# A four-block sequence model on one core: elementwise products on another engine, 512 weight columns per matmul, parameter rows in another order

## The chip, the cores and the metric

The kernel runs on one core of a Trainium2 chip. The core has a matrix engine (TensorE, PE in the rows; its weight loads are PEld), a vector engine (VectorE, DVE), an activation engine (ScalarE, ACT), a general engine (GpSimd, POOL) and SyncE (SP), which here only issues transfers. Each engine has a queue of its own and takes its instructions in order; engines wait for one another by semaphores. SBUF is the on-chip memory that all of them read; TensorE writes its results to PSUM, a second, smaller memory. The metric is the device time of one execution in microseconds.

## What is computed

The input `x` is 256 tokens of 1024 features, in fp32. It goes through two blocks of a first kind and two of a second; all weights are fp32 and are read from HBM once. The reference, cut to its core:

```python
# first kind, for i in 0, 1
proj = rmsnorm(x, norm_mix[i]) @ w_in[i]             # q k v cb cc cx u g
y_attn = sliding_window_attention(q, k, v, sinks) @ w_attn_o[i]
y_conv = (cb * short_conv(cc * cx, conv_w[i])) @ w_conv_o[i]
ys = gelu(s5_ssm(u, ...));  y_ssm = (ys * sigmoid(ys @ w_ssm_glu[i])) @ w_ssm_o[i]
x = x + (g0 * y_attn + g1 * y_conv + g2 * y_ssm) @ w_mix_o[i]
x = x + (silu(gt) * up) @ w_ffn_out[i]               # gt, up = rmsnorm(x) @ w_ffn_in[i]
# second kind, for l in 0, 1
u = rmsnorm_2(h, norm_mix_w[l]) @ w_in[l]            # q k v g_ret z xbc dt gate_ret gate_ssd
yr = retention(rotary(q), rotary(k), v);  o_ret = (silu(g_ret) * norm(yr)) @ ret_out[l]
xs, bm, cm = split(silu(causal_dwconv(xbc)))
lmat[i, j] = exp(acs[i] - acs[j]) for j <= i         # acs: running sum of dt * a
y = ((cm @ bm.T) * lmat) @ (xs * dt) + (state part) + d_skip * xs
o_ssd = (norm(y * silu(z)) * ssd_norm_w) @ ssd_out[l]
h = h + (sigmoid(gate_ret) * o_ret + sigmoid(gate_ssd) * o_ssd) @ w_o[l]
h = h + (silu(gate) * up) @ w_down[l]                # swiglu
# at the end: rmsnorm_2(h, final_norm_w)
```

## The kernel before

Every large product is made of three products of a reduced format (fp32r): weights and activations are each split into a high part and the rest (`wh`, `wl`; `xh`, `xl`, or `hh`, `hl` and the like), and `wh*xh + wh*xl + wl*xh` is summed in PSUM. Weights stream in chunks of 512 KB (`chunk`): SP issues the transfer into one of four `raw` buffers, ACT copies it to `wh` (L121 in the rows, the line of the activation helper), DVE subtracts to get `wl` (L96, the line of the two-tensor helper; L108 is that of the scalar-tensor-tensor helper `stt`). There are five buffers for the split weights.

Two functions make the products. `fm` gives a feature-major result: 128 weight columns are loaded into the array, the 256 tokens stream past. `tm` gives a token-major result: 128 tokens are loaded into the array and the weight columns stream past, 256 of them at a time. In the rows a `tm` matmul reads `mm<-wh,xh`, an `fm` matmul `mm<-xh,wh`, and both have an output of 128x256. In PSUM there are four `mm` buffers of 128x512 values for these and three `ax` buffers of the same size for all else. `tm` makes, in the first blocks, k and v (one product) and q; in the second blocks v and the gate `sg` of each of the four retention heads, `z` of each of the four groups of the SSD stage, and the last FFN product in `output`.

Small chains (rotations, attention, retention heads, the SSD groups' tails, the state-space tables) are generators that `bg.tick()` advances between products. A scheduler then sets the final order of each engine's queue from the dependences, so what is written in a row need not stand in a row.

The SSD stage runs once per second block, over four groups: two `fm` products for `xs`, one `tm` pair for `z` (its silu is `silu2`, L1066), `cb_step` (L1297), the gate product, `xd_step` (L1307) and, later, `group_tail`. `cb_step` multiplies the mask `cbm` into the two decay matrices `Lm` (each 128 x 4 x 384) of the group on POOL; ACT has made these by exponentials before. `xd_step` turns `xs` with TensorE transposes (L1315) into PSUM (`px`), copies that to SBUF with ACT, and has POOL multiply it by dt (`xd`) and by d_skip (`xD`). POOL thus works from SBUF only.

Parameters: `s5_params` loads four small arrays for the state space on ACT's queue at the start. `more_params` is called from `early2` in the first block, after the k/v product: it loads four sets of rows on SP's queue, each followed by a transpose (L190) and a copy into `vec` (L191). The products of the first block need `gfirst` alone at the start; the conv, the gates and the sinks need the rows.

`output` makes the last product in four parts of 256 columns. For each part DVE adds the residual (`xt`), ACT sums squares, POOL multiplies by the gain (`og`); a root on DVE and a last scaling follow.

## Time and profile before

| | us |
|---|---|
| median of 3 runs (2308.11 to 2315.36) | 2312.09 |
| the profiled execution, its span | 2316.8 |
| TensorE busy in it | 2231.6 |
| VectorE busy | 1562.6 |
| ScalarE busy | 1189.4 |
| GpSimd busy | 329.1 |

The span goes from the first to the last instruction of the profiled execution; nothing is measured around it. It stands 4.7 us above the median of the runs. A row of a timeline has the start in us, the duration, engine, line, operation and tiles; a number in square brackets is the time that the engine stood idle before it, with what released it. Rows of matmuls have modelled ends: a matmul's recorded duration is longer than the distance to the next one's start, and it is the distance that counts. Stretches: the first blocks run to about 940 us, the retention and SSD stages of the second blocks at about 950 to 1350 and 1630 to 2050, each followed by its FFN.

### The profile page before, as it was taken

The page shows a single profiled execution, that of the slowest core. Times are in us where ns is not written, and L with a number is a line of the kernel's source. Part 1 is how long each engine was busy: PE and PEld are TensorE (multiplying, and loading weights), DVE is VectorE, ACT ScalarE, POOL GpSimd, SP SyncE. Part 2 cuts the span into 40 slices and gives each one's busy share as a digit, 9 for nine tenths or more (in the row PEclk, how much of TensorE's full clock was granted, in tenths as well). Part 3 has the DMA queues.
Part 4 walks back from the last instruction along what each step waited for, and adds up shares of the span by engine and source line. Part 5 has one row for each costly group of instructions (what it writes and reads, how often), then busy time and mean ns, then how long its engine had stood idle before and what let it go on. Part 6 is the DMA issues. An engine that isn't in the chain of part 4 may idle for free. (4 is left out here: it accounts for less than half of the span.)

```text
span 2316.8 us, 44580 instructions
## 1 busy us (share of the span) xinstructions
PE 2231.6 (96%) x18211; PEld 2199.0 (95%) x18211; DVE 1562.6 (67%) x2533; ACT 1189.4 (51%) x1837; POOL 329.1 (14%) x441
## 2 busy tenths in 40 slices
PE   6899999999999999999999999999999999999998
PEld 6889999999999999999999989999999999989998
DVE  7676686658757665866577867665766577867654
ACT  6556555645555444444476735444444466645443
POOL 5720074101000000100022210000100022310001
PEclk8999999999999999999999999999999999999999
DMA  6333657677456556555576546656555665546553
GB/s 182 119 101 118 184 178 226 221 222 246 140 146 195 182 179 183 164 165 168 161 211 177 150 143 186 183 177 186 161 167 151 196 186 162 152 154 191 182 168 115
DMA packets 409410, 398.27 MB, mean 172 GB/s; under 512 B 28357, under 2 KB 407157, under 8 KB 408181
## 3 DMA queue, kind: packets, MB, share of 16 engines
q1 hardware_dynamic: 408324, 394.59, 56.6%
q8 instruction: 142, 2.33, 0.4%
q10 hardware_dynamic: 880, 0.84, 0.1%
q14 instruction: 64, 0.52, 0.1%
HBM read 386.92 MB, written 8.45 MB: 171 GB/s over the span
## 5 line engine op out<-in xcount | busy, mean ns | idle before, releaser
L96 DVE TENSOR_TENSOR wl<-raw,wh 128x1024 fp32r<-128x1024 f32 (+1 forms) x700 | 890.1, 1274 | 505.8 <-ACT wh L121 501.7
L121 ACT ACTIVATE wh<-raw 128x1024 fp32r<-128x1024 f32 (+1 forms) x700 | 725.8, 1043 | 831.8 <-PE mm L127 706.4
L127 PE MATMUL mm<-xh,wh 128*128 128x256 f32 (+1 forms) x2960 | 850.1, 287 | 3.9 <-ACT wh L121 1.4
L127 PE MATMUL mm<-xl,wh 128*128 128x256 f32 (+1 forms) x2960 | 844.8, 286 | 0.6 <-DVE xl L108 0.6
L127 PE MATMUL mm<-xh,wl 128*128 128x256 f32 (+1 forms) x2960 | 844.3, 285 | 0.2 <-DVE wl L96 0.2
L127 PEld LDWEIGHTS mm<-xh,wh 128*128 128x128 f32 (+1 forms) x2960 | 572.6, 194 | 7.1 <-ACT wh L121 2.3
L127 PEld LDWEIGHTS mm<-xl,wh 128*128 128x128 f32 (+1 forms) x2960 | 572.7, 194 | 2.1 <-issue 1.0
L127 PEld LDWEIGHTS mm<-xh,wl 128*128 128x128 f32 (+1 forms) x2960 | 572.2, 193 | 2.2 <-issue 1.3
L127 PE MATMUL mm<-wh,xh 128*128 128x256 f32 x864 | 252.4, 292 | 0.2 <-DVE tb L96 0.2
L127 PE MATMUL mm<-wh,xl 128*128 128x256 f32 x864 | 246.7, 286 | 5.9 <-DVE xl L108 5.9
L127 PE MATMUL mm<-wl,xh 128*128 128x256 f32 x864 | 245.3, 284 | 0.1
L127 PE MATMUL mm<-y,wh 128*128 128x256 f32 x1024 | 184.5, 283 | 0.0
L127 PEld LDWEIGHTS mm<-wh,xl 128*128 128x128 f32 x864 | 166.8, 193 | 10.1 <-DVE xl L108 7.1
L127 PEld LDWEIGHTS mm<-wh,xh 128*128 128x128 f32 x864 | 166.8, 193 | 3.2 <-issue 1.4
L127 PEld LDWEIGHTS mm<-wl,xh 128*128 128x128 f32 x864 | 166.5, 193 | 0.4 <-DVE wl L96 0.3
L127 PEld LDWEIGHTS mm<-y,wh 128*128 128x128 f32 x1024 | 157.2, 188 | 0.5 <-ACT wh L121 0.4
L96 POOL TENSOR_TENSOR Lm<-Lm,cbm 128x1536 f32<-128x1536 f32 x16 | 65.5, 4114 | 623.4 <-DMA raw<-in_w_in_dram 462.0
L127 PE MATMUL mm<-hh,wh 128*128 128x256 f32 x528 | 148.5, 281 | 0.0
L127 PE MATMUL mm<-hh,wl 128*128 128x256 f32 x528 | 148.1, 280 | 0.0
L127 PE MATMUL mm<-hl,wh 128*128 128x256 f32 x528 | 148.0, 280 | 0.0
L127 PE MATMUL mm<-y,wl 128*128 128x256 f32 x512 | 144.0, 281 | 0.0
L127 PEld LDWEIGHTS mm<-hh,wl 128*128 128x128 f32 x528 | 100.0, 189 | 0.0
(354 smaller groups left out, 3136.7 us busy)
## 6 DMA issues: line engine op xcount, KB each, us to landing
raw<-in_w_in_dram SPq DMA_DIRECT2D x284, 512.0 KB, 3.8
raw<-in_w_ffn_in_dram SPq DMA_DIRECT2D x88, 512.0 KB, 3.7
raw<-in_w_gate_up_dram SPq DMA_DIRECT2D x88, 512.0 KB, 3.6
raw<-in_w_ffn_out_dram SPq DMA_DIRECT2D x40, 512.0 KB, 4.4
raw<-in_w_down_dram SPq DMA_DIRECT2D x40, 512.0 KB, 3.5
raw<-in_ret_out_dram SPq DMA_DIRECT2D x32, 512.0 KB, 4.0
raw<-in_ssd_out_dram SPq DMA_DIRECT2D x32, 512.0 KB, 3.5
raw<-in_w_mix_o_dram SPq DMA_DIRECT2D x16, 512.0 KB, 3.6
```

The source lines that it names most:

```text
L96: return eng.tensor_tensor(out=o, in0=a, in1=b, op=op)
L121: return SC.activation(out=o, in_=i, func=f, **kw)
L127: return PE.matmul(out=o, lhsT=l, rhs=r, start=start, stop=stop)
```

## The change

- `tm` streams 512 weight columns per matmul in place of 256, with two `mm` buffers per product (one per half of the tokens); a chunk for it holds 2 x 512 columns in place of 4 x 256, the same bytes. The k/v product keeps 256. The callers that made two products of 256 make one of 512, and a step of the side chains that stood between the two stands in its middle (`mid`).
- In the SSD stage the `Lm`, `xd` and `xD` products go from POOL to DVE, and `xd` and `xD` read PSUM directly, so the ACT copy goes.
- The first row set and the sinks are loaded at the start, on ACT's queue behind the state-space arrays (`load_params_1`); the three other sets and `drow` later, on SP's queue (`load_params_2`), and they are turned separately (`params_1`, `params_2`).
- High and low parts lie in one tile (`xhl`, `pair`). `silu2` works in place, per token half. `output` makes two parts of 512 columns. In the second blocks the norm's `finish` and the rotation of the first head follow the whole v product, where they stood after its first half.

```diff
-    def more_params(q):
-        for i in range(4):
-            load_rows(i, stg[:, 258 + 128 * i:386 + 128 * i], q)
-        q.dma_start(out=sinks, in_=A["attn_sinks"].partition_broadcast(128))
-        q.dma_start(out=drow, in_=A["d_skip_2"].partition_broadcast(128))
...
+    def load_params_1(q):
...
+        load_rows(0, q)
+        q.dma_start(out=sinks, in_=A["attn_sinks"].partition_broadcast(128))
+    def params_1():
+        turn_rows(0)
...
+    def load_params_2(q):
+        for i in (1, 2, 3):
+            load_rows(i, q)
+        q.dma_start(out=drow, in_=A["d_skip_2"].partition_broadcast(128))
+    def params_2():
+        for i in (1, 2, 3):
+            turn_rows(i)
...
-        for k0 in range(0, KT, 4):
-            kn = min(4, KT - k0)
+        step = 2 if n == 512 else 4
+        for k0 in range(0, KT, step):
+            kn = min(step, KT - k0)
...
-    def tm(w, c0, K, xh, xl, n=256):
-        ps = mmt()
+    def tm(w, c0, K, src, n=512, mid=None):
+        if n == 512:
+            ps = [mmt().rearrange("p a s -> p (a s)") for _ in range(2)]
+        else:
+            both = mmt()
+            ps = [both[:, b, 0:n] for b in range(2)]
...
-                    mmu(ps[:, b, 0:n], h_, wh[:, k, 0:n], kt == 0 and b == 0, False)
-                    mmu(ps[:, b, 0:n], l_, wh[:, k, 0:n], False, False)
-                    mmu(ps[:, b, 0:n], h_, wl[:, k, 0:n], False, kt == KT - 1 and b == 1)
+                    mmu(ps[b], h_, wh[:, k, :], kt == 0 and first, False)
+                    mmu(ps[b], l_, wh[:, k, :], False, False)
+                    mmu(ps[b], h_, wl[:, k, :], False, kt == KT - 1 and last)
+            if mid is not None and k0 + kn == KT // 2:
+                mid()
...
-            for mp in range(4):
-                ps = tm(w_out, mp * 256, FH, hh, hl)
+            for mp in range(2):
+                ps = tm(w_out, mp * 512, FH, hid)
...
             for t in Lms[g]:
-                mul(t, t, bc(cbm, 4), G)
+                mul(t, t, bc(cbm, 4))
...
-                xt = T(tmp, [128, 2, S], "ta").rearrange("p a (h e) -> p (a h) e", e=64)
-                cp(xt, px.rearrange("p (h e) -> p h e", h=8))
-                mul(xd[:, b], xt, bl(dth[:, b, hs], 64), G)
-                mul(xD[:, b], xt, bl(drow[:, l, hs], 64), G)
+                xt = px.rearrange("p (h e) -> p h e", h=8)
+                mul(xd[:, b], xt, bl(dth[:, b, hs], 64))
+                mul(xD[:, b], xt, bl(drow[:, l, hs], 64))
```

The order of the instructions on three engines shows what the diff alone doesn't. A row has the line, the operation, the output and the inputs, the output's size and, on some, the semaphores that it waits for. First TensorE's queue at the v product of the first retention head of the last block, before:

```order
L127 MATMUL mm_19608<-wh_19611,xh_92 128x256
L127 MATMUL mm_19608<-wh_19611,xl_93 128x256
L127 MATMUL mm_19608<-wl_19612,xh_92 128x256
L127 MATMUL mm_19608<-wh_19611,xh_92 128x256
L127 MATMUL mm_19608<-wh_19611,xl_93 128x256
```

And after, the same place; the high and low parts are now in `xhl`, so that two neighbouring rows read alike and are counted as x2:

```order
L127 MATMUL mm_18818<-wh_18821,xhl_92 128x512 x2
L127 MATMUL mm_18818<-wl_18822,xhl_92 128x512
L127 MATMUL mm_18818<-wh_18821,xhl_92 128x512 x2
L127 MATMUL mm_18818<-wl_18822,xhl_92 128x512
L127 MATMUL mm_18819<-wh_18821,xhl_92 128x512 x2
```

The product before is 48 such rows of 256 columns and then 48 more for the other 256; after, it is 48 of 512, and it alternates between two PSUM buffers chunk by chunk.

Second, DVE's queue in an SSD group, between the last two `xs` of the group, before (`ta<-mm,vec,ta` are steps of the convolution, `wl` are weight splits, `sz` is the silu of z):

```order
L108 SCALAR_TENSOR_TENSOR xs_3261_22201<-tb_22348,ta_22339 128x512 [waits Activation_49]
L108 SCALAR_TENSOR_TENSOR sz_22200<-tb_22412,mm_22351 128x2x256 [waits Activation_49]
L96 TENSOR_TENSOR cbm_22491<-ax_22488,B2C 128x384 [waits PE_49]
L96 TENSOR_TENSOR wl_22651<-raw_22647,wh_22650 128x1024 [waits DMAHW7_49,DMAHW0_49,Activation_49]
L108 SCALAR_TENSOR_TENSOR ta_22476<-mm_22415,vec,ta_22476 128x255 [waits Activation_49]
L108 SCALAR_TENSOR_TENSOR ta_22476<-mm_22415,vec,ta_22476 128x254 [waits DVE_49]
L108 SCALAR_TENSOR_TENSOR ta_22476<-mm_22415,vec,ta_22476 128x253 [waits DVE_49]
L96 TENSOR_TENSOR wl_22682<-raw_22678,wh_22681 128x1024 [waits DMAHW1_49,DMAHW2_49,PE_49,Activation_49]
```

And after, from behind `cbm` to the last `xs` (here the `sz` rows belong to the group before, and `nt`, `ny` are two-element steps of a root):

```order
L108 SCALAR_TENSOR_TENSOR ta_21638<-mm_21577,vec,ta_21638 128x253 [waits DVE_49]
L96 TENSOR_TENSOR nt_21685<-nt_21685,nv_21682 128x2 [waits DVE_49]
L96 TENSOR_TENSOR Lm_21650<-Lm_21650,cbm_21704 128x1536 [waits DVE_49]
L108 SCALAR_TENSOR_TENSOR ny_21684<-nt_21685,ny_21684 128x2 [waits DVE_49]
L96 TENSOR_TENSOR Lm_21666<-Lm_21666,cbm_21704 128x1536 [waits DMAHW6_49,DMAHW5_49,Activation_49]
L108 SCALAR_TENSOR_TENSOR ta_21638<-mm_21577,vec,ta_21638 128x255 [waits Activation_49]
L111 TENSOR_SCALAR sz_21002<-sz_21002,ny_21684 128x512 [waits DVE_49]
L108 SCALAR_TENSOR_TENSOR ta_21638<-mm_21577,vec,ta_21638 128x254 [waits DVE_49]
L111 TENSOR_SCALAR sz_21002<-sz_21002,ny_21684 128x512
L108 SCALAR_TENSOR_TENSOR ta_21638<-mm_21577,vec,ta_21638 128x253 [waits DVE_49]
L96 TENSOR_TENSOR wl_21776<-raw_21774,wh_21775 128x1024 [waits DMAHW2_49]
L108 SCALAR_TENSOR_TENSOR xs_3203_21393<-tb_21647,ta_21638 128x512 [waits Activation_49]
```

The two `Lm` products now stand between the steps of the last convolution, ahead of a weight split and of the last `xs`.

Third, ACT's queue at the start, before:

```order
L198 DMA stg<-in_ssm_d_dram 32x4x32 [waits DMAHW1_49]
L121 ACTIVATE xh_92<-mm_150,gfirst 128x256 [waits DVE_49,PE_49]
L121 ACTIVATE xh_92<-ax_151,gfirst 128x256 [waits PE_49]
L121 ACTIVATE xh_92<-mm_152,gfirst 128x256 [waits PE_49]
L121 ACTIVATE xh_92<-mm_150,gfirst 128x256 [waits DVE_49]
L121 ACTIVATE wh_124<-raw_122 128x1024 [waits DMAHW6_49]
```

And after, from behind the same transfer to the first `xh`:

```order
L188 DMA stg<-in_norm_mix_dram 16x128 [waits DMAHW3_49]
L188 DMA stg<-in_norm_ffn_dram 16x128 [waits DMAHW4_49]
L188 DMA stg<-in_norm_final_dram 8x128 [waits DMAHW5_49]
L121 ACTIVATE wh_122<-raw_121 128x1024 [waits DMAHW6_49]
L188 DMA stg<-in_b_gate_dram 48x128 [waits DMAHW7_49]
L188 DMA stg<-in_conv_w_dram 24x128 [waits DMAHW1_49]
L121 ACTIVATE wh_128<-raw_127 128x1024 [waits DMAHW2_49]
L188 DMA stg<-in_norm_mix_w_dram 16x128
L206 DMA sinks<-in_attn_sinks_dram 128x16 [waits DMAHW4_49]
L121 ACTIVATE wh_146<-raw_145 128x1024 [waits DMAHW6_49]
L121 ACTIVATE wh_152<-raw_151 128x1024 [waits DMAHW0_49]
L121 ACTIVATE xhl_92<-mm_160,gfirst 128x256 [waits DVE_49,PE_49]
```

Seven transfers and four weight copies now stand ahead of the first high part of the input.

## Rows read from the trace of the kernel before

**Rows 1.** The page: busy time, share of the span, instructions of each engine.

```profile
PE 2231.6 (96%) x18211; PEld 2199.0 (95%) x18211; DVE 1562.6 (67%) x2533; ACT 1189.4 (51%) x1837; POOL 329.1 (14%) x441
```

**Rows 2.** TensorE's line L127, token-major matmuls of one product: durations, first and last start.

```profile
L127 PE MATMUL mm<-wh,xh x864: 276/283/681, 25.5 to 2023.2; 128*128 128x256 f32 x173
...
L127 PE MATMUL mm<-wh,hh x176: 278/283/365, 2242.0 to 2305.8; 128*128 128x256 f32 x176
```

**Rows 3.** The chain, 1660 to 1680 us: start, length, what, how many.

```profile
1669.99 5.75 PE mm L127 x48
1675.74 1.72 PE ax L127 x4
```

**Rows 4.** TensorE's timeline, 1891 to 1894.6 us; 13 rows like these lie between.

```profile
1891.31 0.41 PE L127 MATMUL mm<-xh,wh 128*128 128x256 f32 x1
...
1894.30 0.41 PE L127 MATMUL mm<-xh,wl 128*128 128x256 f32 x1
```

**Rows 5.** TensorE's waits: engine, line, releaser: us in total, times, longest.

```profile
PE ax L1315 <- DVE xs L108: 29.4, 8, 5.5
PE ax L190 <- DVE vec L191: 10.3, 1, 10.3
```

**Rows 6.** TensorE's timeline, two of the `xs` transposes, three groups apart.

```profile
1890.23 0.44 PE L1315 MATMUL ax<-C,xs 128*128 128x128 f32 x2 [2.69 <-DVE xs L108]
...
2033.40 0.69 PE L1315 MATMUL ax<-C,xs 128*128 128x128 f32 x2 [5.32 <-DVE xs L108]
```

**Rows 7.** Windows, start and SSD: length, busy PE, PEld, DVE, ACT, POOL, PEclk, DMA.

```profile
0.00:150.00 150.00, 120.48 (x862) 115.19 (x862) 110.37 (x281) 83.70 (x154) 89.66 (x185) 0.89 0.47 137
1200.00:1350.00 150.00, 136.53 (x1102) 135.46 (x1101) 118.72 (x182) 93.56 (x173) 46.55 (x23) 0.95 0.56 162
1850.00:2050.00 200.00, 184.06 (x1488) 182.89 (x1487) 151.20 (x235) 127.48 (x237) 53.25 (x24) 0.96 0.57 164
```

**Rows 8.** Timelines of DVE and of POOL, 1878 to 1892 us.

```profile
1878.99 0.55 DVE L96 TENSOR_TENSOR cbm<-ax,B2C 128x384 f32<-128x384 f32 x1
1879.46 1.21 DVE L96 TENSOR_TENSOR wl<-raw,wh 128x1024 fp32r<-128x1024 f32 x1
...
1882.02 3.11 DVE L96 TENSOR_TENSOR wl<-raw,wh 128x1024 fp32r<-128x1024 f32 x1
...
1879.67 8.81 POOL L96 TENSOR_TENSOR Lm<-Lm,cbm 128x1536 f32<-128x1536 f32 x2 [231.43 <-DMA raw<-in_w_in_dram]
```

**Rows 9.** DVE's groups by form: busy, mean ns of one, idle before.

```profile
L96 DVE TENSOR_TENSOR xD<-ax,xD 128x512 f32<-128x512 f32 x16 | 11.0, 686 | 5.8 <-PE ax L127 5.8
```

**Rows 10.** Timelines at the start: ACT's queue and ACT, then DVE, then TensorE.

```profile
5.19 0.44 ACTq L198 DMA_DIRECT2D stg<-in_ssm_d_dram  x1
7.68 0.47 ACT L121 ACTIVATE xh<-mm,gfirst 128x256 fp32r<-128x256 f32 x1 [5.00 <-PE mm L1434]
...
9.26 1.05 ACT L121 ACTIVATE wh<-raw 128x1024 fp32r<-128x1024 f32 x1
...
42.67 0.28 DVE L191 COPY vec<-ax 128x128 f32<-128x128 f32 x1
...
43.00 0.42 PE L190 MATMUL ax<-C,stg 96*128 96x96 f32 x1 [10.34 <-DVE vec L191]
...
88.50 0.44 PE L127 MATMUL ax<-xs,W 128*128 128x64 f32 x1 [5.03 <-DVE xs L96]
```

**Rows 11.** DMA issues, 0 to 14 us: KB each, median us to landing.

```profile
stg<-in_ssm_a_re_dram ACTq DMA_DIRECT2D x1, 16.0 KB, 5.4
```

**Rows 12.** TensorE's timeline in the head of the last block.

```profile
1643.13 0.39 PE L127 MATMUL mm<-wh,xl 128*128 128x256 f32 x1 [1.81 <-DVE xl L108]
```

**Rows 13.** Timelines of DVE and POOL behind the last matmul.

```profile
2306.34 0.88 DVE L108 SCALAR_TENSOR_TENSOR xt<-mm,r,xt 128x256 f32<-128x256 f32 x2 [11.39 <-PE mm L127]
...
2310.78 0.16 DVE L108 SCALAR_TENSOR_TENSOR ny<-nt,ny 128x2 f32<-128x2 f32 x1
...
2307.29 1.26 POOL L96 TENSOR_TENSOR og<-xt,gain 128x512 f32<-128x512 f32 x1 [12.96 <-DVE xt L108]
```

More of the change, by code (lines that the diff above doesn't have):

```diff
@@ L87, in body, with mmt @@
     dramp = pool("dramp", 1, DRAM)
-    def mmt(shape=(128, 2, 256)):
-        return T(mm, list(shape), "mm")
+    def mmt():
+        return T(mm, [128, 2, 256], "mm")
     def axt(shape=(128, 2, 256)):
@@ L188, in load_rows, with turn_rows @@
             r0 += n
+    def turn_rows(i):
+        vr = stg[:, 258 + 128 * i:386 + 128 * i]
+        r0 = sum(n for _, _, n in rows[i])
         pt = axt([128, 512])
@@ L926, in layer1 @@
         bg.tick(next(steps))
[L927 removed]
+        ps = tm(w, 512, D, XX, 256)
         for b in range(2):
             r = nm.rsc[:, b:b + 1]
[L930 to L931 removed]
+            cp(k_tok[:, b].rearrange("p m g e -> p (m g e)"), ps[b][:, 0:128], r)
+            cp(v_tok[:, b, :], ps[b][:, 128:256], r)
         bg.tick(next(steps))
[L933 to L934 removed]
+        if l == 0:
+            params_1()
         r8 = T(sm, [128, 2], "r8")
         ts(r8, nm.rsc, 0.125, None, ALU.mult, ALU.bypass)
[L937 to L942 removed]
+        ps = tm(w, 0, D, XX, mid=lambda: bg.tick(next(steps)))
+        for b in range(2):
+            for g in range(2):
+                cp(q_tok[:, b, :, g, :], ps[b][:, 256 * g:256 * g + 256].rearrange("p (m e) -> p m e", m=4), r8[:, b:b + 1])
         nm.rescale(V if l == 0 else G)
@@ L1053, in layer1 @@
             pst.close()
+            params_2()
         else:
@@ L1066, in silu2 @@
     def silu2(ps, o):
-        b = T(tmp, [128, 2, S], "tb")
-        act(b, ps, AF.Tanh, scale=0.5)
-        stt(o, b, 1.0, ps, ALU.add, ALU.mult)
+        for b in range(2):
+            act(o[:, b], ps[b], AF.Tanh, scale=0.5)
+            stt(o[:, b], o[:, b], 1.0, ps[b], ALU.add, ALU.mult)
     def layer2(l, nm, nxt):
@@ L1231, in layer2 @@
                 bg.tick()
-            for c in range(2):
-                ps = tm(w, 2048 + 512 * h + 256 * c, D, XH, XL)
-                for b in range(2):
-                    cp(v[:, b, 256 * c:256 * c + 256], ps[:, b, :], nm.rsc[:, b:b + 1] if h == 0 else None)
-                if h == 0 and c == 0:
-                    nm.finish()
-                    mul(rcos, B2C[:, 384:640], nm.rsb)
-                    mul(rsin, B2C[:, 640:896], nm.rsb)
-                    rotary(pq, *tabs, e["qT"])
-                    rotary(pk, *tabs, e["kT"])
-                bg.tick()
+            ps = tm(w, 2048 + 512 * h, D, XX, mid=bg.tick)
+            for b in range(2):
+                cp(v[:, b, :], ps[b], nm.rsc[:, b:b + 1] if h == 0 else None)
+            if h == 0:
+                nm.finish()
+                mul(rcos, B2C[:, 384:640], nm.rsb)
+                mul(rsin, B2C[:, 640:896], nm.rsb)
+                rotary(pq, *tabs, e["qT"])
+                rotary(pk, *tabs, e["kT"])
+            bg.tick()
             if h == 0:
@@ L1247, in layer2 @@
             sg = e["sg"] = T(r2, [128, 2, 512], "sg")
-            for c in range(2):
-                silu2(tm(w, 4096 + 512 * h + 256 * c, D, XH, XL), sg[:, :, 256 * c:256 * c + 256])
-                bg.tick()
+            silu2(tm(w, 4096 + 512 * h, D, XX, mid=bg.tick), sg)
+            bg.tick()
             bg.add(head_tail(h))
@@ L1427, in body @@
     norm = Norm(gfirst)
-    xps = [(axt if k2 % 2 else mmt)() for k2 in range(4)]
+    xps = [axt() if k2 % 2 else mmt() for k2 in range(4)]
     for k2 in range(4):
@@ L1443, in body @@
         norm.squares(k2)
-    s5_params(nc.scalar)
+    nc.sync.dma_start(out=B1C, in_=A["cst1"])
+    s5_params()
     s5p = None
@@ L1448, in body @@
     spill = [T(dramp, [128, 3584], f"spill{b}") for b in range(4)]
-    def early2():
-        more_params(nc.sync)
-        nc.sync.dma_start(out=B1C, in_=A["cst1"])
     nxt = Norm(col("norm_mix", 8, 8))
-    layer1(0, norm, nxt.pair, early2)
+    layer1(0, norm, nxt.pair)
     norm = Norm(gfm, gf2)
```

229 lines of the change are left out of this document (111 added, 118 removed).

## The prediction

> **What bounds the kernel now.** I read the busy shares first [rows 1]: TensorE (PE) is busy 2231.6 of 2316.8 us, VectorE (DVE) 1562.6, GpSimd (POOL) 329.1. An engine at 96% sets the end, so the change can pay in three ways only: fewer TensorE microseconds, fewer TensorE stalls, or less time at TensorE's lower clock. The list of TensorE's waits says where it stalls [rows 5]: 29.4 us in 8 stalls at L1315, the transposes in the SSD stage that turn `xs`; and 10.3 us in one stall at L190, the parameter transposes at the start. The windows say where the clock sinks [rows 7]: mean granted clock 0.89 over the first 150 us, 0.95 and 0.96 in the two SSD stretches. The chain gives the pace of the products [rows 3]: 48 matmuls of 256 columns in 5.75 us, 119.8 ns each.
>
> The profiled execution has a span of 2316.8 us, 4.7 us (0.2%) over the median of 2312.1. I take differences from the trace and set them against the median. About 0.3% (7 us) is what a measurement of this kernel can tell from no change.
>
> **512 weight columns.** The token-major matmuls of before stand in two groups of rows, 864 and 176 for one of their three split products [rows 2]; 32 of these 1040 belong to the k/v product, which keeps its width. So 3 x 1008 = 3024 matmuls of 256 columns become 1512 of 512, and 1512 weight loads go. Two old ones cost 239.6 ns. What does one new one cost? The trace has no such matmul in this format, so I bound it. Upper end: 239.6, if the time is proportional to columns; saving 0. A middle: 119.8 is 13 ns more than 256 columns need at 2.4 GHz (106.7). If those 13 ns were a fixed price per matmul, the new one costs 226.5; saving 1512 x 13.1 = 20 us. Lower end: a plain fp32 matmul of 512 columns takes 430 ns [rows 3], which is 1024 columns at full rate and 3 ns, so one pass of 512 columns takes 215; saving 37.2 us. I take 216, by the nearest row: while the granted clock is at its lower level, the same 256-column matmuls stand 213.6 ns apart (14 intervals from 1891.31 to 1894.30 [rows 4]), and 256 columns at 1.2 GHz are 213.3. So a matmul that streams for 213 ns shows no 13 ns on top; they appear only where the stream is short, so they look like something beside the stream, such as the next weight load, that a longer stream hides. A 512-column matmul at full clock streams for the same 213 ns, and has one weight load as well. 1512 x (239.6 - 216) = **-36 us**, on the path, because TensorE is the bound where these products stand (v, gate and q products, the z product of the SSD stage, the last FFN product). Cover: a weight chunk is now eaten in 12 x 216 = 2.6 us instead of 2.9, and its split costs DVE 1.21 us [rows 8].
>
> The Trainium skill ("TensorE: Matmul & The Clock Gate", section "Back-to-back issue gap") gives an isolated gap of N/2.4 + 2.5 ns, which is 109 for 256 columns and 216 for 512; by it the widening would save 1512 x 2.5 = 4 us. The trace disagrees at 256 columns: 119.8 [rows 3]. The same section gives a sustained 131 ns for 512 columns; by that estimate it would save 164 us and the time would be near 2126. No row here streams 512 columns in less than 215.
>
> **Products moved from POOL to DVE.** Per SSD group (8 of them) DVE takes over two `Lm` products of 128x1536 and four of 128x512 that read PSUM. DVE has no 128x1536 row. 128x384 takes 0.55 and 128x1024 takes 1.21 [rows 8], about 1.03 ns per further column, so 1.75; the upper bound is 2.1, three instructions of 512 columns. A 128x512 product from PSUM takes 0.686 [rows 9]. Added: 2 x 1.75 + 4 x 0.69 = 6.2 us per group, 50 us in all. It comes back in part: while POOL runs its two `Lm` products (8.81 us from 1879.67), a DVE split beside them takes 3.11 instead of 1.21 [rows 8]; two fall there, which is 3.8 us per group, and I add 0.7 for what runs beside POOL's `xd` and `xD`. Net +1.7 us per group. DVE is busy 151.2 of 200 us in the second stretch [rows 7], 36.1 per group; a group lasts (2033.40 - 1890.23)/3 = 47.7 us [rows 6]. After: about 38 us of DVE in a group in which TensorE's own work is 47.7 - 3.7 (stall) - 1.6 (half clock) = 42.4, less 1.1 for the wider z product: DVE still fits, at nine tenths.
>
> What the stalls are: DVE finishes the last `xs` late, because its slow splits stand ahead of it in its queue, and TensorE waits 5.32 us at 2033.40 [rows 6]; on average 3.7. After, those splits run at 1.2 us; on the other hand the two `Lm` products stand in the same queue, ahead of the last `xs` and of a split for the z product. I walk the new order from the end of the last `xs` product. DVE owes about six convolution steps (256 columns, some 0.45 each by the 384-column row), two `xs`-like products of 0.69, `cbm`, two `Lm`, two passes over `sz` (0.5 each) and a split: 2.7 + 1.4 + 0.55 + 3.5 + 1.0 + 1.2 = 10.3 us until z's fourth chunk is split. TensorE wants it after three chunks of 2.6 us and the other small work between, near 8.6: a stall of about 2. The `xs` transposes stand later and find their input ready. So 3.7 becomes 2: 29.4 becomes 16. The new wait of DVE's second `Lm` is on ACT's exponentials, and splits queue behind it. The half-clock time is 0.05 x 150 x 2 + 0.04 x 200 x 2 = 31 us in both stretches [rows 7], which loses about 13 us after what fell into stalls; the clock falls after each stall, so with half the stalls I let it lose 6. Gain 13.4 + 7 = **-20 us**. Bounds: -42 (stalls and half clock all gone) and +5 (each stall keeps its length and DVE's net 1.7 us per group lands on TensorE half the time). The 16 copies that ACT no longer makes, and POOL's idleness, are worth nothing by themselves: neither engine is waited for there.
>
> **Parameter rows first.** The L190 stall (10.34 us at 43.00) ends when DVE reaches a copy that it issued at 42.67 behind the tables of the state space [rows 10]; four transposes want PSUM slots there. After, one row set is turned there, three later. That frees up to 10 us. Against it: ACT's queue now has seven more DMA issues and four weight copies ahead of the first `xh`, which before ran at 7.68 [rows 10]. One of the last issues waits for one of the first of the new ones to land; that one goes out some 0.5 us after the last old one of 5.19 [rows 10], and such a small load takes up to 5.4 us to land [rows 11], so it is there near 11; with two weight copies of 1.05 behind the waiting issue [rows 10] the first `xh` runs near 13 to 14, and the first products end some 6 us later. Behind both stands POOL's chain of tables, which feeds the stall of 5.03 us at 88.50 [rows 10] whatever TensorE does before. So most of what is freed is waited away at 88.50: I take **-3 us**, bounds -12 and +6. Loading the other rows later costs seven issues on SP, ahead of transfers that wait for free weight buffers anyway: nothing, or 3 us if a buffer is free.
>
> **The rest.** Heads of the second blocks: the v product now runs whole before the norm's statistics are finished, so the rotary tables and the `xl` chain behind it, whose largest stall (1.81 us) ends at 1643.13 [rows 12], start about 5 us later, with as much more product ahead of them; 0, bounds -3 and +5 per layer. The tail: after the last matmul DVE's `xt` (0.88 for two at 2306.34) and ACT's square double in width, about +0.5; POOL's `og` doubles from 1.26 to 2.5 us but starts near 2307.1 and ends before the root is there at 2310.9 [rows 13]: **+0.5**, bounds 0.4 and 2. Pairs in one tile and the new order of the dt products: nothing, since the same instructions wait for the same halves.
>
> Sum: -36 - 20 - 3 + 0.5 = -58.5, so **2253.6 us** (2258 by the profiled span).
>
> **The rivals.**
> (a) The wider matmul saves nothing: 239.6 is a limit per column, or the weight stream keeps the old pace of 2.9 us a chunk, so that the change doesn't do what it says. Then -22.5: 2289.6. For it: proportional time is the simplest reading of [rows 3]. Against it: [rows 4]. Chance 0.12. The isolated gap of the Trainium skill, cited above, would end near it, at 2286 by that estimate.
> (b) The SSD stage is freed wholly, -42, and the start gains 8: -36 - 42 - 8 + 0.5 = -85.5, 2226.6. For it: both stall and clock hang on one late instruction. Against it: DVE at nine tenths, in order. Chance 0.11.
> (c) **Slower: DVE becomes the bound of the SSD stage.** If its splits stay at 3 us for another reason than POOL, or the added 6.2 us stand in series with what TensorE waits for, each group lasts 47.7 + 6.2 us: +50 - 36 - 3 + 0.5 = +11.5, 2323.6. It decides from a group of 47.7 + 36/8 = 52 us on, that is, when stalls grow from 3.7 to over 8 us. For it: today's largest stall is already DVE's, and idle time of an in-order queue can't be used at will. Against it: the unslowed splits of [rows 8]. Chance 0.09.
> (d) The start or the two heads lose what is bounded above, about 9 us: 2262.6. Chance 0.11.
>
> **How the numbers follow.** The forecast has 0.53; 0.04 is left for mixtures of (a) and half of (c), which end within 0.3% of before. Faster by over 0.3%: 0.53 + 0.12 + 0.11 + 0.11 = 0.87; same 0.04; slower 0.09. The range goes from (b), 2226, to just above (a), 2292; left out are the 0.13 above and some 0.05 below.
>
> **What will show it.** Right: 48 matmuls of 512 columns in 10.4 us of the chain (a: 11.5; fixed price: 10.9). SSD groups of 43 to 45 us with splits at 1.2 us and no stall at the `xs` transposes above 2 us; a clock of 0.97 or more there. Slower side: stalls on `wl` or `Lm` in the SSD stage, groups above 50 us. Start: no 10 us stall at the parameter transposes, first `xh` near 14 us, and the stall on POOL's chain grown. What would break the sum: a clock that falls in the retention stage, where it is full now.

## The result, and the profile after

The changed kernel takes 2276.85 us (median, 2274.23 to 2277.81), the kernel before 2311.72 in the same session: a ratio of 0.9845, 95% interval 0.9831 to 0.9860, or 35.8 us at the 2312 us of before. The forecast was 58.5 us. The direction held and the time lies in the range, but four terms of the sum were off, three one way and one the other. The profiled execution after has a span of 2274.2 us, so the two traces stand 42.6 us apart, 7 us more than the medians; for sizes below I take ratios of medians, and the traces for places.

The page's first line, and TensorE's longest waits (us in total, times, longest), answering [rows 1, 5]:

```profile
PE 2208.2 (97%) x16699; PEld 2110.4 (93%) x16699; DVE 1567.2 (69%) x2573; ACT 1181.9 (52%) x1795; POOL 212.3 (9%) x391
```

```profile
PE mm L127 <- ACT xhl L121: 14.0, 4, 7.4
PE ax L127 <- DVE dg L111: 9.1, 3, 7.2
PE mm L127 <- DVE xhl L108: 5.6, 4, 1.9
```

The 29.4 us at the `xs` transposes are gone from the list altogether; so is the stall at the parameter transposes. In their place stand longer waits for the high part of the activations (`xhl` from ACT; 1.3 us before) and for `dg`, the broadcast of a norm's statistics (2.3 us before); the waits for the low part, `xhl` from DVE, were there before too (6.5 us in 7). The windows of the start, of a head of a second block and of the SSD stages (length, busy PE, PEld, DVE, ACT, POOL, then PEclk, DMA) answer [rows 7]:

```profile
0.00:150.00 150.00, 118.64 (x795) 110.17 (x796) 112.61 (x273) 82.66 (x151) 85.23 (x185) 0.90 0.45 134
940.00:970.00 30.00, 24.02 (x107) 19.43 (x106) 24.54 (x48) 13.21 (x20) 5.49 (x4) 0.83 0.40 123
1200.00:1330.00 130.00, 130.00 (x969) 123.47 (x968) 116.00 (x203) 88.46 (x162) 0.00 (x0) 1.00 0.58 179
1850.00:2000.00 150.00, 148.71 (x1077) 139.60 (x1076) 133.37 (x226) 101.56 (x185) 0.00 (x0) 1.00 0.57 175
```

Both SSD stretches run at full clock with TensorE busy 99% or more. The head of the second block (second row) does not: 0.83. Before, that window read:

```profile
940.00:970.00 30.00, 26.92 (x219) 26.26 (x218) 27.62 (x52) 14.63 (x24) 6.26 (x4) 1.00 0.43 123
```

The `xs` transposes on TensorE's timeline stand without an idle time in brackets, 41.9 and 42.8 us apart, where [rows 6] had 47.7 us and stalls up to 5.3:

```profile
1869.56 0.60 PE L1343 MATMUL ax<-C,xs 128*128 128x128 f32 x4
...
1911.42 0.60 PE L1343 MATMUL ax<-C,xs 128*128 128x128 f32 x4
...
1954.24 0.60 PE L1343 MATMUL ax<-C,xs 128*128 128x128 f32 x4
```

The chain at a retention head (start, length, what, how many) gives the price of the new matmul, 24 of 512 columns in 5.49 us, 228.8 ns each with the ends of the stretch. That is 10.98 us for 48, the prediction's sign of a fixed price (10.9):

```profile
1655.63 5.49 PE mm L127 x24
```

Lengths of stages in the two traces, each from the first matmul of a kind to the first of the next:

| stretch | before, us | after, us |
|---|---|---|
| start to the state space's GLU product in the first block | 184.7 | 187.2 |
| from there to the FFN-down product of the second block | 679.9 | 678.6 |
| third block: from that FFN-down on, head, retention | 251.2 | 252.8 |
| `ret_out` and SSD stage | 237.9 | 216.2 |
| `ssd_out`, mix, FFN-up | 198.0 | 197.7 |
| fourth block: FFN-down of the third, head, retention | 250.2 | 251.7 |
| `ret_out` and SSD stage | 241.6 | 217.9 |
| `ssd_out`, mix, FFN-up | 198.5 | 199.6 |
| last product | 64.0 | 60.5 |

All of the gain stands in three rows: the two SSD stages, 21.7 and 23.7 us, and the last product, 3.5 us. The two retention stretches hold half of all 512-column matmuls, and both got longer.

### The profile page after: what moved, and what is told of

Its sections match the earlier page's. It is cut to its first block, busy times and chain, and to the rows that moved or that the text cites. A ratio compares the mean times of both kernels' runs of the same rounds, so it can differ in the third digit from the quotient of the medians.

```text
span 2274.2 us, 41403 instructions
## 1 busy us (share of the span) xinstructions
PE 2208.2 (97%) x16699; PEld 2110.4 (93%) x16699; DVE 1567.2 (69%) x2573; ACT 1181.9 (52%) x1795; POOL 212.3 (9%) x391
## 5 line engine op out<-in xcount | busy, mean ns | idle before, releaser
L127 PE MATMUL mm<-xhl,wh 128*128 128x256 f32 x5920 | 1087.4, 285 | 15.0 <-ACT xhl L121 8.2
L127 PEld LDWEIGHTS mm<-xhl,wh 128*128 128x128 f32 x5920 | 926.6, 192 | 21.4 <-ACT xhl L121 8.9
L127 PE MATMUL mm<-xhl,wl 128*128 128x256 f32 (+1 forms) x2960 | 841.2, 284 | 0.4 <-DVE wl L96 0.4
L127 PEld LDWEIGHTS mm<-xhl,wl 128*128 128x128 f32 (+1 forms) x2960 | 568.5, 192 | 1.9 <-issue 0.8
L127 PE MATMUL mm<-wh,xhl 128*128 128x512 f32 (+1 forms) x896 | 280.8, 397 | 9.0 <-ACT xhl L121 5.8
L127 PEld LDWEIGHTS mm<-wh,xhl 128*128 128x128 f32 x896 | 168.8, 193 | 47.3 <-ACT xhl L121 6.2
L127 PE MATMUL mm<-hh,wh 128*128 128x256 f32 x1056 | 188.1, 281 | 0.0
L127 PE MATMUL mm<-y,wh 128*128 128x256 f32 x1024 | 184.6, 283 | 0.0
L127 PE MATMUL mm<-wl,xhl 128*128 128x512 f32 (+1 forms) x448 | 174.7, 393 | 0.0
L127 PEld LDWEIGHTS mm<-hh,wh 128*128 128x128 f32 x1056 | 162.4, 189 | 0.0
L127 PEld LDWEIGHTS mm<-y,wh 128*128 128x128 f32 x1024 | 157.5, 188 | 0.9 <-ACT y L121 0.4
L127 PE MATMUL mm<-hh,wl 128*128 128x256 f32 x528 | 148.1, 280 | 0.0
L127 PE MATMUL mm<-y,wl 128*128 128x256 f32 x512 | 143.9, 282 | 0.0
L127 PEld LDWEIGHTS mm<-wl,xhl 128*128 128x128 f32 x448 | 86.3, 193 | 17.3 <-DVE wl L96 0.2
L127 PEld LDWEIGHTS mm<-hh,wl 128*128 128x128 f32 x528 | 100.0, 189 | 0.0
L127 PEld LDWEIGHTS mm<-y,wl 128*128 128x128 f32 x512 | 96.2, 188 | 0.0
L127 PE MATMUL mm<-mg,wh 128*128 128x256 f32 x512 | 91.2, 281 | 0.0
L127 PEld LDWEIGHTS mm<-mg,wh 128*128 128x128 f32 x512 | 78.6, 188 | 0.0
```

The source lines that it names most:

```text
L127: return PE.matmul(out=o, lhsT=l, rhs=r, start=start, stop=stop)
```

## The experiments

### One part at a time

**SSD products alone.** The kernel before, with these lines changed and nothing else:

```diff
-                mul(t, t, bc(cbm, 4), G)
+                mul(t, t, bc(cbm, 4))
...
-                xt = T(tmp, [128, 2, S], "ta").rearrange("p a (h e) -> p (a h) e", e=64)
-                cp(xt, px.rearrange("p (h e) -> p h e", h=8))
-                mul(xd[:, b], xt, bl(dth[:, b, hs], 64), G)
-                mul(xD[:, b], xt, bl(drow[:, l, hs], 64), G)
+                xt = px.rearrange("p (h e) -> p h e", h=8)
+                mul(xd[:, b], xt, bl(dth[:, b, hs], 64))
+                mul(xD[:, b], xt, bl(drow[:, l, hs], 64))
```

> The kernel before, with the SSD products alone (Lm, xd, xD) on VectorE. Theory now (the SSD move carries nearly the whole gain: the two SSD stages got 21.7 and 23.7 us shorter between the traces, of which about 4 us are the wider z product): 41 us faster, near 2271, with no stall at the xs transposes and groups of about 42.5 us. Theory of the prediction (20 us from this part): near 2292. Rival (VectorE is the new bound, the widening saved the stage): 0 to 10 us slower than before.

Measured: 2280.95 us, ratio 0.9854 (0.9838 to 0.9870), 33.8 us faster. The stall at the `xs` transposes is down to 5.6 us in 2, and the clock in the second SSD stretch is full:

```profile
PE ax L1315 <- DVE xs L108: 5.6, 2, 3.2
```

```profile
1840.00:2000.00 160.00, 157.58 (x1324) 157.17 (x1323) 136.97 (x231) 113.22 (x209) 0.00 (x0) 1.00 0.61 177
```

So this part alone gives nearly the whole net gain, as the theory after the result had it (41 expected, 33.8 measured), and more than the 20 us of the prediction. The slower rival of that run falls.

**512 columns alone.** The changed kernel with the SSD lines above reversed and the parameter rows as before.

> The changed kernel with the SSD products back on GpSimd and the parameter rows loaded as before; what is left of the change is 512 columns and what comes with it (one tile for high and low part, the whole v product before the norm is finished, the output in two parts). Theory now (a 512-column matmul at 227 to 229 ns saves 11 to 13 ns for each two old ones, 1512 times: 16 to 19 us; the heads of the two second blocks give back 5.7 us each): 5 to 8 us faster than before, near 2305. Theory of the prediction (216 ns): 36 us faster, near 2276. Rival (widening has no effect at all): 0, with the heads 11 us slower.

Measured: 2321.7 us, ratio 1.0030 (1.0019 to 1.0041): 7 us slower than before. All three expectations miss. The stalls at the `xs` transposes (29.4 us before) are gone from the list of waits, which names a new place, the transposes of the SSD stage's output, waiting for `sz`:

```profile
PE ax L1371 <- DVE sz L111: 33.0, 6, 5.7
```

and DVE's and POOL's timelines show the reason (start, length, engine, operation):

```profile
1919.42 0.47 DVE L108 SCALAR_TENSOR_TENSOR ta<-mm,vec,ta 128x253 f32<-128x253 f32 x1
1919.81 3.30 DVE L96 TENSOR_TENSOR nt<-nt,nv 128x2 f32<-128x2 f32 x1
1923.03 1.21 DVE L96 TENSOR_TENSOR wl<-raw,wh 128x1024 fp32r<-128x1024 f32 x1
1924.16 3.37 DVE L108 SCALAR_TENSOR_TENSOR ny<-nt,ny 128x2 f32<-128x2 f32 x1
```

```profile
1919.58 7.94 POOL L96 TENSOR_TENSOR Lm<-Lm,cbm 128x1536 f32<-128x1536 f32 x2 [16.83 <-DVE cbm L96]
```

A DVE operation on two elements per partition takes 3.30 us beside POOL's `Lm`, and a second one 3.37; alone such a step takes 0.15 to 0.17. Between the two, DVE's split takes its normal 1.21. Convolution steps, which read one operand from PSUM, aren't slowed: in the kernel before, three of them stand wholly beside the `Lm` products of [rows 8] and take 0.5 us each.

```profile
1885.05 1.50 DVE L108 SCALAR_TENSOR_TENSOR ta<-mm,vec,ta 128x255 f32<-128x255 f32 x3
```

So DVE as a whole isn't slower. The rows read as a DVE instruction with two SBUF operands that waits until POOL's instruction of some 4 us is over: the second one ends at 1927.53, and POOL's pair at 1927.52. The same reading fits [rows 8]: the split that started at 1882.02 took 1.9 us more than its normal 1.2. The Trainium skill says this in "SBUF — State Buffer", section "SBUF: two separate sides": DVE and GpSimd share a port pair, "an exclusive lock, not a bandwidth split", held for the whole instruction, against DVE operations with two SBUF inputs among others. The rows agree: 3.30 us for two elements, 0.5 with one operand in PSUM.

In this kernel the scheduler's new order puts the tiny steps of a root beside POOL's `Lm`, and the whole tail of the group waits for them. The widening and the SSD move are therefore not independent: with the products on GpSimd the widening costs 7 us, and with them on VectorE it gains 9 (0.9815 for the kernel with the rows as before, below, against 0.9854 for the SSD products alone). Both figures hold what the late finish of the norm costs in the heads, which a later run measures at some 15 us.

### What in the SSD move carries the gain

**`Lm` alone**, and **`xd` and `xD` alone**, each in the kernel before; the diffs are the first pair of lines above, and the others.

> The kernel before with the two Lm products of each group alone on VectorE; xd and xD stay on GpSimd with their ScalarE copy. Theory (GpSimd's 8.8 us of Lm per group slowed the weight splits beside it and made the last xs late): most of the 33 us of the run with all three, 24 to 33 us faster than before, near 2285, splits at 1.2 us. Rival (xd and xD, which VectorE can read from PSUM, carried the gain): under 8 us faster.

> The kernel before with xd and xD alone on VectorE, read from PSUM; Lm stays on GpSimd. Theory (the Lm products on GpSimd are the cause): within 5 us of before, splits of 3.1 us and the stalls at the xs transposes still there. Rival (xd and xD carried the gain): 25 us faster.

Measured: `Lm` alone 2297.68 us, ratio 0.9929 (0.9914 to 0.9944), 16 us faster; `xd` and `xD` alone 2314.64, ratio 1.0005 (0.9995 to 1.0015), no change. `Lm` alone gives half of what all three give, which neither theory had. `xd` and `xD` alone do what the first theory said: nothing moves, since the stall stands (the list of waits of that run):

```profile
PE ax L1315 <- DVE xs L108: 28.4, 8, 5.6
```

With `Lm` alone, POOL's four remaining products of a group take 2 us each, one behind the other, and DVE's splits in 1840 to 2000 us still take 1368 ns in the mean, against 1218 when all are moved (POOL's timeline, then DVE's group by form with busy time and mean ns):

```profile
1921.55 1.85 POOL L96 TENSOR_TENSOR xd<-ta,dth 128x512 f32<-128x512 f32 x1 [35.33 <-ACT ta L121]
1923.36 2.02 POOL L96 TENSOR_TENSOR xD<-ta,drow 128x512 f32<-128x512 f32 x1
```

```profile
L96 DVE TENSOR_TENSOR wl<-raw,wh 128x1024 fp32r<-128x1024 f32 x45 | 60.8, 1368 | 15.0 <-ACT wh L121 14.6 <-PE mm L127 0.3
```

So `Lm` left on GpSimd keeps the whole loss, and `xd` and `xD` left there keep half of it; only moving both takes POOL out of the stage. With `Lm` alone TensorE also waits 3.9 us, in 2 stalls, for POOL's `xd` itself, so a part of what is left there is lateness.

**POOL at idle work.** The changed kernel, and beside each `Lm` on DVE a product of the same shape on POOL whose result nothing uses:

```diff
+        idle = T(d1, [128, 4, 384], "idle")
+        G.memset(idle, 0.0)
...
             for t in Lms[g]:
                 mul(t, t, bc(cbm, 4))
+                mul(idle, idle, bc(cbm, 4), G)
```

> The changed kernel with two idle products of 128x1536 per group on GpSimd, started by the same cbm as the Lm products of before; nothing waits for their result. It tells what GpSimd costs by running alone from what it cost by finishing late. Theory (running beside the splits is the cost): splits and VectorE's own Lm beside them rise from 1.2 and 1.75 to 3 us and more, stalls return, 15 to 30 us slower than the changed kernel. Rival (the cost was that TensorE waited for GpSimd's results): within 4 us of the changed kernel.

Measured: 2341.79 us, ratio to before 1.0127 (1.0107 to 1.0147). That is 65 us over the changed kernel, some 8 us per group, twice the most that was expected. In the changed kernel DVE's `Lm` reads (group by form, busy time and mean ns):

```profile
L96 DVE TENSOR_TENSOR Lm<-Lm,cbm 128x1536 f32<-128x1536 f32 x16 | 27.9, 1750 | 0.0
```

and with POOL beside it 2293 ns, while two-element steps rise to 1209 and 1762 ns in the mean (groups of 1840 to 2000 us):

```profile
L96 DVE TENSOR_TENSOR Lm<-Lm,cbm 128x1536 f32<-128x1536 f32 x6 | 13.8, 2293 | 0.0
...
L96 DVE TENSOR_TENSOR nt<-nt,nv 128x2 f32<-128x2 f32 x6 | 7.3, 1209 | 0.1
...
L108 DVE SCALAR_TENSOR_TENSOR ny<-nt,ny 128x2 f32<-128x2 f32 x4 | 7.0, 1762 | 0.0
```

The splits, which were expected to slow, keep 1219 ns in these groups; the cost fell on `Lm`, `xs` and the steps of the root. No result of POOL's idle products is waited for, so lateness isn't needed for a loss: running beside DVE is enough. How the 33.8 us divide between lateness and the lock isn't told by this run, since DVE carries `Lm` too in it.

### The price of a matmul

**Widths.** The changed kernel with five streams of 48 matmuls behind the last product, in the split format; the results are unused. In the first stream DVE, ACT, GpSimd and some transfers still work on the end of the program; in the four others they are idle (their busy times in the windows below no longer grow):

```diff
+            f0, f1 = hid(0), hid(2)
+            mv = f1.rearrange("p a s -> p (a s)")
+            for n, wd in ((512, 128), (384, 128), (256, 128), (128, 128), (512, 32)):
+                pz = mmt().rearrange("p a s -> p (a s)")
+                for j in range(48):
+                    st_ = f0[:, j % 2, 0:wd]
+                    mmu(pz[0:wd, 0:n], st_, mv[:, 0:n], j == 0, j == 47)
```

> The changed kernel with five streams of 48 matmuls behind its last product, all in the split format: 512, 384, 256 and 128 columns with 128 weight columns, then 512 columns with 32 weight columns. Their results are not used; the time is about 39 us longer. VectorE, ScalarE and the transfers are idle meanwhile. Theory A (a fixed price of 13 to 15 ns per matmul at full clock): 227 to 229, 173, 120 and 67 ns each. Theory B (the price comes from other engines' traffic): 215, 162, 108 ns. Theory C (the weight load of 128 columns is the floor of about 120 ns): 512 and 384 at 215 and 162, 256 and 128 both at 120; and a 32-column load brings 512 to 213.

The run took 2308.37 us, in one execution. The windows all begin at 2263.50; the count behind PE busy is that of the matmuls begun (the first two belong to the last product), so two windows of one stream give a pace. They end behind the 6th and the 48th begun, the 54th and 96th, the 102nd and 144th, the 148th and 190th, the 200th and 242nd:

```profile
2263.50:2264.28 0.78, 0.78 (x6) 0.62 (x5) 0.26 (x1) 0.67 (x2) 0.00 (x0) 1.00 0.00 0
2263.50:2273.80 10.30, 10.30 (x48) 8.51 (x47) 5.33 (x17) 2.73 (x6) 2.40 (x1) 1.00 0.27 99
2263.50:2275.06 11.56, 11.56 (x54) 9.61 (x53) 5.33 (x17) 2.73 (x6) 2.40 (x1) 1.00 0.24 91
2263.50:2282.36 18.86, 18.86 (x96) 16.91 (x95) 5.33 (x17) 2.73 (x6) 2.40 (x1) 1.00 0.15 56
2263.50:2283.30 19.80, 19.80 (x102) 17.85 (x101) 5.33 (x17) 2.73 (x6) 2.40 (x1) 1.00 0.14 53
2263.50:2288.32 24.82, 24.82 (x144) 22.87 (x143) 5.33 (x17) 2.73 (x6) 2.40 (x1) 1.00 0.12 43
2263.50:2288.80 25.30, 25.30 (x148) 23.35 (x147) 5.33 (x17) 2.73 (x6) 2.40 (x1) 1.00 0.11 42
2263.50:2293.44 29.94, 29.94 (x190) 27.99 (x188) 5.33 (x17) 2.73 (x6) 2.40 (x1) 1.00 0.10 36
2263.50:2295.02 31.52, 31.52 (x200) 29.09 (x198) 5.33 (x17) 2.73 (x6) 2.40 (x1) 1.00 0.09 34
2263.50:2304.76 41.26, 41.26 (x242) 33.67 (x241) 5.33 (x17) 2.73 (x6) 2.40 (x1) 1.00 0.07 26
```

| columns, weight columns | ns per matmul (42 intervals) | over columns / 2.4 GHz |
|---|---|---|
| 512, 128 | 9.52 / 42 = 226.7 | 13.3 |
| 384, 128 | 7.30 / 42 = 173.8 | 13.8 |
| 256, 128 | 5.02 / 42 = 119.5 | 12.9 |
| 128, 128 | 4.64 / 42 = 110.5 | 57.1 |
| 512, 32 | 9.74 / 42 = 231.9 | 18.6 |

Theory A holds from 256 columns on: a fixed 13 ns per matmul, whether other engines work (119.8 [rows 3]) or not (119.5). At 128 columns it fails: 110.5 and not 67, so something else sets the time there. Theories B and C fall; with 32 weight columns the 512-column stream was even slower, in this one stream. By an estimate from its formula, the Trainium skill's isolated gap ("TensorE: Matmul & The Clock Gate", section "Back-to-back issue gap") would be 216, 162 and 109 ns; the measured times in this format are 10 to 11 ns longer, and the measurement decides.

### The head and the start

**The norm's finish in the middle of the v product.** The changed kernel, with a step of before put back:

```diff
-            ps = tm(w, 2048 + 512 * h, D, XX, mid=bg.tick)
+            def half():
+                if h == 0:
+                    nm.finish()
+                    mul(rcos, B2C[:, 384:640], nm.rsb)
+                    mul(rsin, B2C[:, 640:896], nm.rsb)
+                    rotary(pq, *tabs, e["qT"])
+                    rotary(pk, *tabs, e["kT"])
+                bg.tick()
+            ps = tm(w, 2048 + 512 * h, D, XX, mid=half)
...
-            if h == 0:
-                nm.finish()
-                mul(rcos, B2C[:, 384:640], nm.rsb)
-                mul(rsin, B2C[:, 640:896], nm.rsb)
-                rotary(pq, *tabs, e["qT"])
-                rotary(pk, *tabs, e["kT"])
```

> The changed kernel, but in the head of each second block the norm's finish, the tables and the rotation of the first head are issued in the middle of the v product, as before the change. Theory now (5.7 us per layer are lost because the chain behind the norm starts after the whole product, and the clock falls in the gaps): 8 to 11 us faster than the changed kernel, near 2267, stalls in the head under 4 us per layer and no clock drop there. Rival (the loss belongs to the 512-column product itself, or to the gate product that follows): the same as the changed kernel, 2277.

Measured: 2264.86 us, ratio to before 0.9781 (0.9764 to 0.9798). Against the changed kernel that is 0.0064 of 2312, 14.8 us, more than was expected. The head's window has TensorE busy 28.30 and a clock of 0.94, where no drop was expected:

```profile
940.00:970.00 30.00, 28.30 (x151) 24.31 (x150) 26.98 (x66) 14.55 (x22) 6.97 (x4) 0.94 0.45 128
```

In the changed kernel the chain behind the norm began with the whole v product already done, so three stalls stood in the head. Two of the last block's (TensorE's timeline):

```profile
1623.89 0.53 PE L127 MATMUL mm<-wh,xhl 128*128 128x512 f32 x1 [3.43 <-ACT xhl L121]
...
1628.51 0.79 PE L127 MATMUL mm<-wh,xhl 128*128 128x512 f32 x1 [1.61 <-DVE xhl L108]
```

Behind them the clock was at its lower level: 12 intervals of 512 columns in 5.12 us, 426.7 ns each, which is 512 / 1.2 GHz with nothing on top.

```profile
1629.10 0.63 PE L127 MATMUL mm<-wl,xhl 128*128 128x512 f32 x1
...
1634.22 0.81 PE L127 MATMUL mm<-wh,xhl 128*128 128x512 f32 x2
```

**Parameter rows as before**, in the changed kernel; **both** undone; and **the first set early, but on SP's queue** behind the first four weight chunks:

```diff
-        load_rows(0, q)
-        q.dma_start(out=sinks, in_=A["attn_sinks"].partition_broadcast(128))
...
     prefetch(A["w_in"][0], 2560, D)
+    load_rows(0, nc.sync)
+    nc.sync.dma_start(out=sinks, in_=A["attn_sinks"].partition_broadcast(128))
```

The diff is that of the third of these, without the edit at the v product, which it has too; the first of them puts `more_params` back, and the second does that and the edit at the v product.

> The changed kernel with the parameter rows loaded and turned as before (all on the SP queue after the k/v product). Theory now (the start lost 2.5 us: first high part of the input at 16.7 instead of 7.7 us, and a new stall of 7.2 us at the norm's broadcast): 2 to 3 us faster than the changed kernel, near 2274, which may not be told from no change; the 10 us stall at the parameter transposes is back and the 7.4 us stall at the first product is gone. Theory of the prediction: 3 us slower than the changed kernel, near 2280.

> The changed kernel with both losses undone: the norm's finish in the middle of the v product, and the parameter rows loaded as before. Theory (the two losses, 12 us and 4.5 us, lie in different stages and add): 16 us faster than the changed kernel, near 2260. Rival (they overlap): no better than the run with the finish alone, 2265.

> The changed kernel with the norm's finish in the middle of the v product; the first row set and the sinks are loaded early, as in the change, but on the SP queue behind the first four weight chunks, so that ScalarE's queue starts with the high parts of the input. Theory (the start lost by ScalarE's queue waiting for the row transfers, and the single early transpose is worth something): first high part near 8 us, no 10 us stall at the parameter transposes, 2 to 6 us faster than with the rows as before, near 2256. Rival (GpSimd's chain of tables bounds the start whatever comes first): the same as with the rows as before, near 2260.

| kernel | us | ratio to before, interval |
|---|---|---|
| changed | 2276.85 | 0.9845 (0.9831 to 0.9860) |
| rows as before | 2272.40 | 0.9815 (0.9796 to 0.9834) |
| finish in the middle | 2264.86 | 0.9781 (0.9764 to 0.9798) |
| both | 2258.03 | 0.9751 (0.9735 to 0.9768) |
| finish in the middle, rows on SP | 2256.17 | 0.9751 (0.9735 to 0.9766) |

The early rows cost 0.0030 of 2312, 7 us, in both pairs of kernels that differ by it. The intervals of each pair overlap at their ends, so the size is uncertain by a few us; the sign rests on two pairs that agree. The start of the changed kernel shows how (ACT's timeline, then TensorE's):

```profile
10.84 1.02 ACTq L206 DMA_DIRECT2D sinks<-in_attn_sinks_dram  x1
14.20 1.06 ACT L121 ACTIVATE wh<-raw 128x1024 fp32r<-128x1024 f32 x1 [2.67 <-DMA raw<-in_w_in_dram]
15.70 1.06 ACT L121 ACTIVATE wh<-raw 128x1024 fp32r<-128x1024 f32 x1 [0.44 <-DMA raw<-in_w_in_dram]
16.66 0.46 ACT L121 ACTIVATE xhl<-mm,gfirst 128x256 fp32r<-128x256 f32 x1
```

```profile
17.17 0.80 PE L127 MATMUL mm<-xhl,wh 128*128 128x256 f32 x2 [7.39 <-ACT xhl L121]
...
48.04 0.58 PE L127 MATMUL ax<-dg,C 128*128 128x128 f32 x1 [7.21 <-DVE dg L111]
```

The first high part comes at 16.66 where it came at 7.68 [rows 10]: two weight copies stand ahead of it that wait for chunks landing as late as 14 to 15.7 us. With the rows on SP it comes at 7.91 and the time is that of "both" to within the measurement. So the rival of that run holds in its number: getting the rows earlier is worth nothing that can be measured, and what cost was ACT's queue. The rows of the start show another reason than the one that the rival named, GpSimd's chain. The stall of some 10 us is only moved: with both undone it stands at the parameter transposes, and with the rows on SP at a weight split (TensorE's waits, one line of each run, then DVE's timeline of the second):

```profile
PE ax L195 <- DVE vec L196: 9.5, 1, 9.5
```

```profile
PE mm L127 <- DVE wl L96: 9.5, 3, 9.0
```

```profile
44.98 1.22 DVE L96 TENSOR_TENSOR wl<-raw,wh 128x1024 fp32r<-128x1024 f32 x1
```

Either way TensorE waits for what DVE reaches behind its steps for the state-space tables, 42.67 in [rows 10] and 44.98 here. Both last kernels beat the changed one by some 20 us, 2.5% under before.

## Why the prediction was right or wrong

By ratios, at 2312 us, the change takes apart as follows; the second column is the prediction's term. Each part is the step from one measured kernel to another, so the parts add up by construction, and each is uncertain by some 5 us.

| part | predicted | measured | from |
|---|---|---|---|
| SSD products to DVE | -20 | -33.8 | SSD products alone |
| 512 columns, without the heads' loss | -36 | -23.8 | "both" against SSD alone |
| heads of the second blocks | 0 | +14.8 | finish in the middle |
| parameter rows | -3 | +7 | "both" against finish in the middle |
| sum | -58.5 | -35.8 | |

The parts hold for this order of steps. Put in behind the widening, the SSD move is worth 49.7 us (512 columns alone, 1.0030, against the kernel with the rows as before, 0.9815), since the 33.0 us of waits for `sz` go with it (3.1 are left).

The time lies well inside the range in part by luck: three terms promised 12, 15 and 10 us too much, and the SSD term 14 too little. With 20 us from the SSD stage, as forecast, the time would have been near 2290, at the upper end.

The sum of the prediction has +0.5 for the tail too. From the last matmul's start to the span's end it was 10.8 us before and is 12.1 after, in single executions. The step that failed there is that POOL's `og` costs nothing because it ends before the root is there. The first step of that root, on two elements per partition, ends with `og`, and `og` is now twice as long (DVE before and after, then POOL after; POOL before is in [rows 13]):

```profile
2307.86 0.71 DVE L96 TENSOR_TENSOR ssq<-ssq 128x2 f32<-128x2 f32 x1 [0.65 <-ACT sq L121]
```

```profile
2264.09 1.65 DVE L96 TENSOR_TENSOR ssq<-ssq 128x2 f32<-128x2 f32 x1 [0.79 <-ACT sq L121]
2263.38 2.34 POOL L96 TENSOR_TENSOR og<-xt,gain 128x1024 f32<-128x1024 f32 x1 [27.52 <-DVE xt L108]
```

**512 columns: the step that failed is "I take 216".** The price was bounded rightly, 215 to 239.6, and the middle, 226.5 by a fixed 13 ns, was the measured one (226.7). I moved to the lower end on [rows 4]: at the lower clock 256 columns take 213.6 ns with nothing on top, so a matmul that streams 213 ns at full clock should show nothing on top either. The inference went from time to time, and the price goes with the clock: at the lower level 512 columns take 426.7 with nothing on top, at the higher one every width from 256 on pays 13 ns. Saved per new matmul: 239.6 - 226.7 = 12.9 ns, 19.5 us in all, not 36. The retention stretches of the kernel with the finish in the middle are 4.8 and 6.7 us shorter than before, against 384 x 12.9 = 5.0 by the price, and the last product 3.5 against 264 x 12.9 = 3.4. Of the other 4 us of the 23.8, nearly 3 stand in the SSD stages: with both undone these are 7.7 us shorter than with the SSD products alone, against 5.0 by the price, and the 5.6 us of stalls left at the `xs` transposes are gone. The rest is within the measurement.

**Heads: the step that failed is "start about 5 us later, with as much more product ahead of them; 0".** The bound of +5 per layer named the mechanism and I took the wrong end: it was 7 per layer. The half product moved ahead of the chain doesn't cover the chain; it was cover behind it that had gone, and the gate product had to wait for the rescaled `xl` either way. The price was above the bound because the stalls brought the clock down, which the sum had priced in the SSD stage only: in the last block's head the stalls come to 6.6 us, against 1.6 with the finish in the middle, and the retention stretch is 8.3 us longer. The last sentence of the prediction named a falling clock in the retention stage as what would break the sum, and it fell in that stage's head.

**SSD stage: right mechanism, term too small by 14 us.** DVE's `Lm` takes 1750 ns as estimated, DVE is busy 133.4 of 150 us there, nine tenths as worked out, and no stall at the transposes is left. What failed is the 2 us of stall that I kept per group: it was not there (the waits list has 0.4 us on `wl` for the whole program, once), and the clock is full. The prediction let the clock fall after each stall; in the trace before it fell behind seven of the eight. The relief was undercounted too: beside POOL's `xd` and `xD` I took 0.7 us per group, and those products alone keep half of the loss when `Lm` is gone. Rival (b) had this stage at -42; the measured value lies between.

**Parameter rows: the step that failed is the -3 between bounds of -12 and +6.** The first high part was put at 13 to 14 us and came at 16.66. The waiting issue was rightly put near 11 (10.84), but the two weight copies behind it were taken at 1.05 us each, without the wait for their chunks (2.67 and 0.44 us in ACT's rows). The 10 us that the sum counted as freed were not to be had: the stall belongs to DVE's steps for the tables and not to the transposes, as the run with the rows on SP shows. In the changed kernel 7.39 us stand at the first product and 7.21 at the norm's broadcast in its place. The second of them did come from POOL's chain of tables, near 48 us and not at 88.50: the split ahead of the broadcast needs a copy that stood in ACT's queue behind this wait (ACT's timeline):

```profile
43.29 1.69 ACT L121 ACTIVATE BX<-BP 64x256 f32<-64x256 f32 x4 [8.16 <-POOL BP L96]
```

Rival (d) had named these two losses, of the start or of the heads, at about 9 us; both came, at 15 and 10 us against the sum's terms. Rival (a) falls: the wider matmul saves 12.9 ns for each two old ones.

The slower rival (c) had no part: the measured DVE share is the predicted one and it fits. With idle GpSimd products beside it, the kernel did end slower than before, at 2341.79.

## What to carry to other kernels

Two engines that share a lock don't share work: moving a product off GpSimd pays by what GpSimd no longer holds up on VectorE, and a part of the move can be worth nothing until the rest is moved (`xd` and `xD` alone: no change). Price a wider instruction by its own clock level, with the fixed part kept, until a stream of it has been timed. When a half product becomes a whole one, ask what was issued between the halves; the chain behind it loses its cover, and a stall can cost more than its length through TensorE's clock (5.0 us more of stalls made one retention stretch 8.3 us longer). When a stall goes, ask what its releaser holds up next: a stall that hangs on an engine's queue moves to the next thing in that queue.

## What the runs showed of the hardware

The fixed 13 ns per matmul at the higher clock level and its absence at the lower one (213.6 for 256 and 426.7 for 512 columns) weren't expected; why it is absent there stays open. Nor was it expected that 32 weight columns in place of 128 make a 512-column stream slower (231.9 against 226.7 ns, one stream each), or that a two-element VectorE step can take 3.4 us beside GpSimd, as three kernels show (512 columns alone, GpSimd at idle work, and the changed kernel's tail with 1.65).
